# A hybrid decoder layer on one core: the z gates of its linear attention through memory, and joined runs of tile work in its sparse attention

## The chip, the core and the metric

The kernel runs on one core of a Trainium2 chip. The metric is the device time of one execution, in microseconds (us), as the median of several runs.

## What is computed

One step of a decoder layer for 320 tokens: a prompt of 256 and 8 samples of 8 tokens each. The samples have a past of 2048 keys, in caches of 16 pages of 128 keys. Cut to its core, the reference is

```python
u = rmsnorm(x, norm_g) @ w_in                      # 2048 -> 23664 columns, split below
# mixer A, linear attention (gated delta rule): 16 q/k heads, 32 v heads, head dim 128
q, k, v = split(silu(causal_conv4(qkv, conv_state)))
o, s    = gated_delta_chunked(l2norm(q) / 128 ** .5, l2norm(k), v, beta, g, s0)   # chunks of 64 tokens
o_a     = rmsnorm(o, gdn_norm_g) * silu(z)                                        # z: 32 heads
# mixer B, sparse attention: 16 query heads in 4 groups, three kinds of keys, gates g per head
o_cmp   = softmax(q . rmsnorm(compress(k_cmp)) + bias) @ compress(v_cmp)          # pooled blocks of 32, stride 16
o_sel   = softmax(q . k_sel + bias, the 16 best blocks of 64) @ v_sel
o_win   = softmax(q . k_win + bias, last 512 keys) @ v_win
o_b     = (g0 * o_cmp + g1 * o_sel + g2 * o_win) * silu(z_b)
y       = x + (sigmoid(m_a) * (o_a @ w_branch_a) + sigmoid(m_b) * (o_b @ w_branch_b)) @ w_out
```

The new keys and values, the convolution's tails and the states s are outputs too.

## The kernel before

**The projection as filler.** The weight products are most of the work. Each weight tile is split in two parts, whi (a copy rounded to the fast matmul type, on ACT) and wlo (weight less whi, on DVE). A tile of 128 columns over one k-tile of 128 rows then takes three matmuls into the PSUM tile acc, all 320 tokens wide: hhi by whi, hlo by whi, hhi by wlo (hhi and hlo are the two parts of the normed input). With 16 k-tiles a block of 128 columns is 48 of them.

The blocks stand in a queue Q of "slabs", filled by slab(). Four streams serve it, each strictly in order: p_load (the weights' DMAs on SP, three buffers wraw), p_hi, p_lo and p_mm (the matmuls on PE). Each slab has a condition ready: p_mm starts no block until it holds, and what stands behind in Q waits with it. At a block's end a function of the slab takes acc away: take_raw and take_mz copy it to a buffer raw (ACT; four of them, counted by room), and take_mz writes that to memory from POOL's queue; take_g copies it to xp, the convolution's input.

The order of Q is: the heads' gates (bag), q, the six kinds of keys and values, the gates z_b, m_a, m_b (take_mz, to d_mz), half of the z gates (the 16 heads listed in ZS: take_mz, to d_z), and then for each pair j of v heads (j = 0 to 15) a slab of q and k columns, one of v columns and, for j > 0, one of the pair's z columns that are not in ZS. Last come three slabs of m_b, then w_branch_b, w_branch_a and w_out.

**Who sets the order.** Everything else is a set of Python generators (prepare, prompt, compressed, window, two workers of sample, and for each j the streams of the linear attention). Each yields the engine and tiles that it needs next. A planner (Clock and Run) keeps modelled engine times and lets the stream step that can start first; at equal times the rank decides. p_mm has the highest number for a rank: its matmuls come where no other stream can run on PE. So the program order of every engine is fixed when the kernel is built, and at run time each engine works through its row in order. All instructions are recorded by one helper (L330; the DMAs at L298), so the profile's groups are told apart by tiles.

**The linear attention.** For each j: conv (the xp tiles to cv), load_z (reads z_b and the z heads in ZS, line 1616), norms (silu of q, k, v and z; transposes), prep and inverse (the chunks' triangular inverses: long chains of products of 32x32 tiles, ps by T, X, A and TTd), then g2 (the four prompt chunks) and g3 (the samples, which read and write states sS of all 8 sequences: matmuls pu, writes o_s_gdn). pos["g2"] and pos["g3"] count the pairs that are through. The tile z has three buffers. The matmul for the z columns of pair j goes straight into that tile (take_g of kind "z"), so its slab has the condition of line 1597:

```python
okz = lambda f, j=j: pos["g2"] >= j - 2 and pos["g3"] >= j - 2
```

The q/k and v slabs have another, ok: at most four xp tiles at a time.

**The sparse attention.** Part of PE's work here uses a part of its array: tiles of 128 rows by 32 columns (four groups of heads side by side), 64 by 32, 64 by 128 or 32 by 32. A matmul of the projection uses 128 by 128. pooled (line 1158) takes four pages of the compressed cache at a time and multiplies each by the weights Pk to 32 rows of pp: a run of 7 instructions, then three of 4. scores (1291) transposes pages of keys (nt, copied to kT) and multiplies them by the queries: 4 instructions ns for a page, two pages at a time in sample and one in window; after the pages come 4 for the sample's new keys. weighted (1312) does the same with the transposed probabilities pT and pages of values (op), the new values last, from vsS or vwS with 64 rows. In prompt (997) each head's transposed pooled probabilities pcT have 64 rows, and the matmul with vcp uses 64 of the array's rows.

Of the kernel before, what the change touches and what calls it, by code (L numbers as in the profile page):

```python
# [21 lines left out]
P = 128  # L22
# [3 lines left out]
B = 8  # L26
# [16 lines left out]
NWP = 5  # L43
# [392 lines left out]
def step(ctx: ExitStack, tc: tile.TileContext, I, O):  # L436
# [32 lines left out]
    d_z = dpool.tile([len(ZS), P, NT], F32, name="d_z")  # L469
# [328 lines left out]

    room = lambda f: done["taken"] - done["raw"] < NRAW
# [8 lines left out]
    for x in mz[:24 - NM]:  # L808
        w_in(*x)
    for i in range(0, len(ZS), 2):  # L810
        w_in([(OZA + 128 * j, 128) for j in ZS[i:i + 2]], take_mz(d_z, i))
# [20 lines left out]
    vcp = wtab.tile([64, 4, P], F32, name="vcp")  # L832
# [131 lines left out]
    def prompt_compress(tok):  # L964
        V.memset(kcpT, 0.0)
        V.memset(vcp, 0.0)
        for kv, nm in enumerate(("kc", "vc")):
# [22 lines left out]
            else:  # L990
                vp = wps.tile([P, 512], F32, tag="b", name="vp")
                for g in range(4):
                    T.matmul(vp[:32, g * P:g * P + P], pt[:, g * 32:g * 32 + 32], proj[:, 1], start=True, stop=True)
                yield "dve"
                V.tensor_copy(vcp[:32].rearrange("p g d -> p (g d)"), vp[:32])

    def prompt():
        yield lambda: done["names"]
        qp = {}
        for g, tt in ((g, tt) for g in range(4) for tt in range(2)):  # L1000
# [32 lines left out]
            for h in range(4):  # L1033
                T.transpose(tp[:64, h * P:h * P + P], pc[:, h], ident)
            yield "act"
            pcT = wk.tile([64, 512], F32, tag="wpcT", name="pcT")
            S.activation(pcT, tp[:64], AF.Copy)
            ob = wk.tile([P, 4, P], F32, tag="wob", name="ob")
            for h in range(4):
# [38 lines left out]
                T.matmul(op[:, :P], vcp[:, g], pcT[:, h * P:h * P + P], start=False, stop=True)  # L1078
# [73 lines left out]
    cfeed = Feed(cp, "cpg", 6, [page(key, b, 4 * j + i) for b in range(B) for key in ("k_cmp", "v_cmp")  # L1152
# [5 lines left out]
    def pooled(b, kv):  # L1158
        pp = cps.tile([P, 512], F32, tag="a", name="pp")
        for i in range(4):  # L1160
            pg = []
            for _ in range(4):
                pg.append((yield from cfeed.get()))
            yield ("pe", *pg)
            for j in range(4):
                T.matmul(pp[32 * j:32 * j + 32], Pk[:, kv, i], pg[j], start=i == 0, stop=i == 3)
# [3 lines left out]
            cfeed.release(4)  # L1170
# [66 lines left out]
    def select(h):  # L1237
# [17 lines left out]
        for a in (0, 15):  # L1255
            big = cp.tile([P, 2, 450], F32, tag="big", name="big", bufs=1)
            mine, other = bc(sc[:, a:], [[1, 15], [0, 30]]), bc(sc, [[0, 15], [1, 30]])
            v = [big[:, k].rearrange("p (a b) -> p a b", a=15) for k in range(2)]
# [13 lines left out]
    class Env:  # L1272


        def __init__(self, pp, st, tt, nt, pl, n, i, feed):
            self.feed, self.next, self.nt = feed, Next(pp, tt), nt
            self.s = lambda name: pp.tile([P, 512], F32, tag=st, name=name)
            self.t = lambda name: pp.tile([P, 512], F32, tag=tt, name=name, bufs=nt)
            self.x = lambda name: pl.tile([P, 512], F32, tag=f"{name}{i}", name=name, bufs=n)
# [11 lines left out]
    def scores(e, b, npg, dst, kS, finish):  # L1291

        for quad in range(0, npg, 4):
            ns = e.s("ns")
            prev = []
            for p in range(0, 4 + e.nt, e.nt):
                got, now = [], []
                if p < 4:
                    for _ in range(e.nt):
                        got.append((yield from e.feed.get()))  # L1300
                    yield ("pe", *got, e.next)
                    for k, pg in enumerate(got):
                        if k:
                            yield ("pe", e.next)
                        nt = e.t("nt")
                        for g in range(4):
                            T.transpose(nt[:, g * P:g * P + P], pg[:, g * P:g * P + P], ident)
                        now.append(nt)
                        e.feed.release()
                if prev:  # L1310
# [1028 lines left out]
```

## Time and profile before

| | us |
|---|---|
| median of 3 runs | 2661.42 |
| lowest and highest | 2658.48, 2663.15 |
| the profiled execution | 2657.93 |
| its span, first to last instruction | 2655.9 |

The page's rows count instructions as the hardware runs them: a float32 matmul of the sparse or linear attention is two records, one of the projection is one. PE stands for the matmuls and PEld for the loads of their weights; a time such as 1467.6 is microseconds from the span's start. In the span, input and norm take the first 30 us, the sparse attention lies between 30 and about 1100, the linear attention between about 1100 and 2229, and after it only projection is left. "clock" is the TensorE clock granted, as a share of full speed; its mean over the execution was 0.988.

### The profile page before, as it was taken

To read this page: it belongs to the slowest core of one execution; us is meant where nothing else is said; L and a number is where in the kernel's file an instruction comes from. 1 tells how busy PE (TensorE), PEld (TensorE's weight loads), DVE (VectorE), ACT (ScalarE), POOL (GpSimd) and SP (SyncE) were. 2 spreads that over 40 slices of the span, in tenths; PEclk is the share of its full clock that TensorE was granted. 3 is DMA by queue.
4 is the path that set the end of the run, shared out by engine and by line. 5 is a ranking of instruction groups with operands and counts; after the bars stand their busy time and mean duration, and the time that the engine had idled before them with its cause. 6 is when DMAs were issued, how large, how long until landed. Compare 5 with 4: busy or idle time off the path is not lost. (4 is left out here: it accounts for less than half of the span.)

```text
span 2655.9 us, 59457 instructions
## 1 busy us (share of the span) xinstructions
PE 2581.8 (97%) x22228; PEld 2332.5 (88%) x22228; DVE 1648.4 (62%) x4089; ACT 1407.7 (53%) x3290; POOL 398.0 (15%) x967
## 2 busy tenths in 40 slices
PE   7999999999999999999999899989999899999999
PEld 5897788777878888899999699979998789999999
DVE  5554445655556555544887787878878776454543
ACT  5453443434433333345778568777777565444443
POOL 2000011000000000000222343324242322000000
PEclk9999999999999999999999899989999899999999
DMA  6747777898768998765546256545464366656654
GB/s 193 232 156 242 232 238 268 273 322 267 252 207 281 316 359 273 242 195 156 153 152 189 88 179 180 163 131 154 145 189 147 122 195 216 208 180 191 184 191 131
DMA packets 548677, 543.89 MB, mean 205 GB/s; under 512 B 32482, under 2 KB 452499, under 8 KB 548003
## 3 DMA queue, kind: packets, MB, share of 16 engines
q1 hardware_dynamic: 534308, 493.67, 58.3%
q0 software_dynamic: 14080, 46.41, 5.1%
q8 instruction: 175, 2.87, 0.4%
q14 instruction: 114, 0.93, 0.1%
HBM read 470.31 MB, written 69.67 MB: 203 GB/s over the span
## 5 line engine op out<-in xcount | busy, mean ns | idle before, releaser
L330 PE MATMUL acc<-hhi,whi 128*128 128x320 f32 (+1 forms) x3472 | 1146.3, 330 | 1.5 <-ACT hhi L330 1.5
L330 PE MATMUL acc<-hhi,wlo 128*128 128x320 f32 (+1 forms) x3472 | 1075.3, 310 | 0.0
L330 PE MATMUL acc<-hlo,whi 128*128 128x320 f32 (+1 forms) x3472 | 1074.1, 309 | 0.5 <-DVE hlo L330 0.4
L330 ACT ACTIVATE whi<-wraw 128x512 fp32r<-128x512 f32 (+1 forms) x996 | 626.2, 630 | 834.5 <-PE acc L330 792.4
L330 DVE TENSOR_TENSOR wlo<-wraw,whi 128x512 fp32r<-128x512 f32 x992 | 685.4, 694 | 576.3 <-ACT whi L330 545.6
L330 PEld LDWEIGHTS acc<-hhi,whi 128*128 128x128 f32 (+1 forms) x3472 | 654.9, 189 | 70.1 <-issue 57.4
L330 PEld LDWEIGHTS acc<-hlo,whi 128*128 128x128 f32 (+1 forms) x3472 | 655.6, 189 | 7.0 <-issue 2.2
L330 PEld LDWEIGHTS acc<-hhi,wlo 128*128 128x128 f32 (+1 forms) x3472 | 653.5, 188 | 0.0
L330 PE MATMUL acc<-oah,whi 128*128 128x320 f32 x512 | 158.2, 309 | 0.0
L330 PE MATMUL acc<-oal,whi 128*128 128x320 f32 x512 | 158.2, 309 | 0.0
L330 PE MATMUL acc<-oah,wlo 128*128 128x320 f32 x512 | 158.2, 309 | 0.0
L330 POOL CAST vx<-v 32x128 fp32r<-32x128 f32 x256 | 97.8, 382 | 143.7 <-DVE v L330 91.5
L298 POOL DMA_DIRECT2D d_mz<-raw x48 | 26.2, 545 | 605.5 <-ACT raw L330 594.1
L330 DVE SCALAR_TENSOR_TENSOR cv<-xp,cw,cv 128x344 f32<-128x344 f32 x192 | 109.9, 573 | 6.0 <-ACT cv L330 4.7
L330 ACT ACTIVATE kT<-nt 128x512 f32<-128x512 f32 x80 | 47.6, 596 | 109.2 <-PE ns L330 63.4
L330 DVE COPY kT<-nt 128x512 f32<-128x512 f32 x80 | 55.1, 690 | 69.7 <-PE ns L330 51.6
L330 PEld LDWEIGHTS acc<-oah,whi 128*128 128x128 f32 x512 | 96.1, 188 | 0.0
L330 PEld LDWEIGHTS acc<-oal,whi 128*128 128x128 f32 x512 | 96.1, 188 | 0.0
L330 PEld LDWEIGHTS acc<-oah,wlo 128*128 128x128 f32 x512 | 96.1, 188 | 0.0
L330 DVE SCALAR_TENSOR_TENSOR sS<-sS,ends,pu 128x128 f32<-128x128 f32 x256 | 82.8, 338 | 19.0 <-PE pu L330 18.1
L330 PE MATMUL pp<-cpg,Pk 128*32 128x512 f32 x608 | 88.0, 602 | 0.8 <-DMA cpg<-cache_k_cmp 0.7
L330 PE MATMUL nt<-pk_const,spg 128*128 128x128 f32 x512 | 68.5, 275 | 1.2 <-DVE kT L330 0.9
(422 smaller groups left out, 3436.3 us busy)
## 6 DMA issues: line engine op xcount, KB each, us to landing
wraw<-w_in SPq DMA_DIRECT2D x136, 1024.0 KB
wraw<-w_in SPq DMA_DIRECT2D x97, 512.0 KB
cpg<-cache_k_cmp SPq DMA_DIRECT2D x128, 256.0 KB
cpg<-cache_v_cmp SPq DMA_DIRECT2D x128, 256.0 KB
spg<-cache_k_sel SPq DMA_DIRECT2D x128, 256.0 KB
spg<-cache_v_sel SPq DMA_DIRECT2D x128, 256.0 KB
wraw<-w_branch_a SPq DMA_DIRECT2D x32, 1024.0 KB
sS<-state_gdn SPq DMA_DIRECT2D x32, 512.0 KB
```

What stands on the lines that cost most here:

```text
L298: return f(*a, **k)
L330: return f(*a, **k)
```

## The change

**The z gates.** d_z has rows for all 32 heads. The 16 heads that are not in ZS are no longer computed into the tile z. They are computed in eight slabs of two heads each, which stand among the q/k and v slabs (the pair 3, 5 behind those of j = 0, 7 and 9 behind j = 2, and so on to 30 and 31 behind j = 14). Their condition is room: fewer than four raw buffers in use. take_z copies acc to raw, POOL writes it to d_z, and zdone notes the head. load_z reads both heads of a pair with one DMA on SP, once g2 and g3 have come to j - 2 and zdone has both; norms takes them from there. The number of projection matmuls is the same.

**Joined runs.** pooled takes eight pages at a time (8 buffers instead of 6) in runs of 11 and 8 instructions, and gives all eight back at the run's end. scores keeps the transposed keys of four pages in sample (two in window) and multiplies them in one run of 16 instructions (8). The new keys of all samples of a worker come first, in new_scores; in sample POOL copies them to xs. weighted multiplies four pages of values in one run of 16, with the new values' four ahead of the first. In prompt, the pooled probabilities of two heads are transposed at once (16 instructions fewer in all), and vcp is laid out twice, in rows 0 to 63 and 64 to 127 with zeros in the other half, so that its matmul uses the whole array (4 matmuls vp more). qp has one buffer instead of two and is loaded when its group begins. The window's pages go from 5 buffers to 4.

The program's matmuls on PE go from 17904 to 17892. Counted in its order, the runs of instructions that use a part of the array (anything but 128 by 128 or 128 by 64) go from 422 to 288: the pooling's from 62 to 31, those of ns from 101 to 55, those of op in sample and window from 73 to 35, those of op by pcT from 24 to none; in the linear attention they go from 118 to 122, and all others from 44 to 45.

The diff, cut to its core:

```diff
@@ -466,7 +466,7 @@
...
-    d_z = dpool.tile([len(ZS), P, NT], F32, name="d_z")
+    d_z = dpool.tile([32, P, NT], F32, name="d_z")
...
@@ -796,6 +796,14 @@
...
+    zdone = set()
+
+    def take_z(heads):
+        def f(ft, acc):
+            yield from take_mz(d_z, heads[ft])(0, acc)
+            zdone.add(heads[ft])
+        return f
+
...
@@ -807,8 +815,9 @@
...
+    z_pair = lambda x: w_in([(OZA + 128 * j, 128) for j in x], take_z(x))
     for i in range(0, len(ZS), 2):
-        w_in([(OZA + 128 * j, 128) for j in ZS[i:i + 2]], take_mz(d_z, i))
+        z_pair(ZS[i:i + 2])
 
     run.add(gain(), -1)
...
@@ -989,10 +998,12 @@
...
-                for g in range(4):
-                    T.matmul(vp[:32, g * P:g * P + P], pt[:, g * 32:g * 32 + 32], proj[:, 1], start=True, stop=True)
+                for i in range(2):
+                    for g in range(4):
+                        T.matmul(vp[64 * i:64 * i + 32, g * P:g * P + P], pt[:, g * 32:g * 32 + 32], proj[:, 1], start=True, stop=True)
...
@@ -1002,10 +1013,9 @@
...
-                for x in range(len(qp), min(g + 2, 4)):
-                    yield ("sp",)
-                    qp[x] = wwin.tile([P, 4, TP], F32, tag="qp", name="qp", bufs=2)
-                    SY.dma_start(qp[x], d_q[x])
+                yield ("sp", Next(wwin, "qp"))
+                qp[g] = wwin.tile([P, 4, TP], F32, tag="qp", name="qp")
+                SY.dma_start(qp[g], d_q[g])
...
@@ -1030,11 +1040,11 @@
...
-            for h in range(4):
-                T.transpose(tp[:64, h * P:h * P + P], pc[:, h], ident)
+            for h in range(2):
+                T.transpose(tp[:, h * P:h * P + P], pc[:, 2 * h:2 * h + 2].rearrange("p h n -> p (h n)"), ident)
             yield "act"
-            pcT = wk.tile([64, 512], F32, tag="wpcT", name="pcT")
-            S.activation(pcT, tp[:64], AF.Copy)
+            pcT = wk.tile([P, 256], F32, tag="wpcT", name="pcT")
+            S.activation(pcT, tp[:, :256], AF.Copy)
...
@@ -1075,7 +1085,7 @@
...
-                T.matmul(op[:, :P], vcp[:, g], pcT[:, h * P:h * P + P], start=False, stop=True)
+                T.matmul(op[:, :P], vcp[:, h % 2, g], pcT[:, h // 2 * P:h // 2 * P + P], start=False, stop=True)
...
@@ -1149,7 +1159,7 @@
...
-    cfeed = Feed(cp, "cpg", 6, [page(key, b, 4 * j + i) for b in range(B) for key in ("k_cmp", "v_cmp")
+    cfeed = Feed(cp, "cpg", 8, [page(key, b, 4 * j + i) for b in range(B) for key in ("k_cmp", "v_cmp")
...
@@ -1157,17 +1167,18 @@
...
-        for i in range(4):
+        for i in range(0, 4, 2):
             pg = []
-            for _ in range(4):
+            for _ in range(8):
                 pg.append((yield from cfeed.get()))
             yield ("pe", *pg)
-            for j in range(4):
-                T.matmul(pp[32 * j:32 * j + 32], Pk[:, kv, i], pg[j], start=i == 0, stop=i == 3)
+            for k in range(8):
+                j = k % 4
+                T.matmul(pp[32 * j:32 * j + 32], Pk[:, kv, i + k // 4], pg[k], start=i + k // 4 == 0, stop=i + k // 4 == 3)
             if i == 0:
                 for j in range(3):
                     T.matmul(pp[32 * j:32 * j + 32], Pk[:, kv, 4], pg[j + 1], start=False, stop=False)
-            cfeed.release(4)
+            cfeed.release(8)
...
@@ -1288,51 +1300,50 @@
...
+    def new_scores(e, bs, kS, dst):
+
+        yield ("pe", e.sum)
+        ns = e.s("ns")
+        for i, b in enumerate(bs):
+            for g in range(4):
+                T.matmul(ns[32 * g:32 * g + 32, 64 * i:64 * i + 64], qT(b, g), kS[:, g], start=True, stop=True)
+        for i, b in enumerate(bs):
+            yield ("dve", ns)
+            V.scalar_tensor_tensor(dst[:, i], ns[:, 64 * i:64 * i + 64], SCALE, newB[:, 56 - 8 * b:120 - 8 * b], op0=OP.mult, op1=OP.add)
...
         for quad in range(0, npg, 4):
-            ns = e.s("ns")
-            prev = []
...
-                    yield ("pe", *got, e.next)
-                    for k, pg in enumerate(got):
...
+            ks, ns = [], None
+            for p in range(4):
+                pg = yield from e.feed.get()
...
+                e.feed.release()
+                ks.append(e.x("kT", e.nk))
...
+                if len(ks) < e.nk:
+                    continue
+                yield ("pe", *ks, *([] if ns else [e.sum]))
+                ns = ns or e.s("ns")
+                for k, kT in enumerate(ks, p + 1 - e.nk):
+                    for g in range(4):
+                        T.matmul(ns[32 * g:32 * g + 32, k * P:k * P + P], qT(b, g), kT[:, g * P:g * P + P], start=True, stop=True)
+                ks = []
...
-        prev = None
-        for quad in list(range(0, npg + 1, 4)) + [None]:
+
+        pend = []
+        for quad in [npg] + list(range(0, npg, 4)) + [None]:
...
@@ -1341,29 +1352,28 @@
...
-            if prev is not None:
...
-                    yield ("pe", *got, pT)
...
-                        for g in range(4):
-                            T.matmul(op[32 * g:32 * g + 32], pT[:m0, c + 32 * g:c + 32 * g + 32], pg[:m0, g * P:g * P + P],
-                                     start=q0 == 0 and k + i == 0, stop=q0 == npg)
-                        if q0 < npg:
-                            e.feed.release()
+            if quad not in (0, npg):
+                got = []
+                for q0, n0, m0, pT in pend:
+                    for k in range(n0):
+                        got.append(((yield from e.feed.get()) if q0 < npg else vS, pT, k, m0))
+                last = quad is None
+                yield ("pe", *[y[0] for y in got], *[y[3] for y in pend])
+                for i, (pg, pT, k, m0) in enumerate(got):
+                    for g in range(4):
+                        T.matmul(op[32 * g:32 * g + 32], pT[:m0, k * P + 32 * g:k * P + 32 * g + 32], pg[:m0, g * P:g * P + P],
+                                 start=pg is vS, stop=last and i == len(got) - 1)
+                e.feed.release(sum(y[0] is not vS for y in got))
+                pend = []
...
-                pT = e.x("pT")
+                pT = e.x("pT", 2 if npg > 4 else 1) if quad < npg else e.new("pTn")
...
-                prev = quad, n, m, pT
+                pend.append((quad, n, m, pT))
...
@@ -1408,8 +1420,10 @@
...
-        env = Env(sps, "s", "t", 2, smp, 2, "", Feed(smp, "spg", n, req))
-        for b in bs:
+        env = Env(sps, "s", "t", 2, smp, 4, Feed(smp, "spg", n, req))
+        xn = smp.tile([P, len(bs), 64], F32, name="xn")
+        yield from new_scores(env, bs, ksS, xn)
+        for i, b in enumerate(bs):
             yield lambda: done["sel"] > b // 4
...
@@ -1426,11 +1440,15 @@
...
-            yield from scores(env, b, 16, xs, ksS, fin_s)
+            yield ("pool", xn, Place(clock, xs))
+            G_.tensor_copy(xs[:, 2048:], xn[:, i])
...
@@ -1572,15 +1590,9 @@
...
-    def take_g(j, kind, f0=0):
+    def take_g(j, kind):
 
         def f(ft, acc):
-            if kind == "z":
-                z = z_of(j)
-                yield ("act", acc)
-                S.activation(z[:, f0 + ft], acc, AF.Copy)
-                pos["z", j] = pos.get(("z", j), 0) + 1
-                return
             t = g1.tile([P, 347], F32, tag="xp", name="xp", bufs=NXP)
...
@@ -1592,14 +1604,14 @@
...
+    zl = [h for h in range(2 * NG) if h not in ZS]
     for j in range(NG):
...
-        okz = lambda f, j=j: pos["g2"] >= j - 2 and pos["g3"] >= j - 2
         slab(I["w_in"], INW, ((OQ + P * j, P), (OK_ + P * j, P)), KT, hhi, hlo, ok, take_g(j, "c"), xp_enter)
         slab(I["w_in"], INW, ((OV + 256 * j, 256),), KT, hhi, hlo, ok, take_g(j, "v"), xp_enter)
-        zh = [h for h in range(2) if 2 * j + h not in ZS]
-        if zh:
-            slab(I["w_in"], INW, ((OZA + 256 * j + 128 * zh[0], 128 * len(zh)),), KT, hhi, hlo, okz, take_g(j, "z", zh[0]))
+        while zl and zl[0] < 2 * j + 4:
+            z_pair(zl[:2])
+            del zl[:2]
...
@@ -1615,20 +1627,16 @@
...
-        early = [h for h in range(2) if 2 * j + h in ZS]
...
         SY.dma_start(ob, d_ob[j])
-        if early:
-            yield lambda: pos["g2"] >= j - 2 and pos["g3"] >= j - 2
-            yield ("sp",)
-            z = z_of(j)
-            for h in early:
-                SY.dma_start(z[:, h], d_z[ZS.index(2 * j + h)])
-            pos["z", j] = pos.get(("z", j), 0) + len(early)
+        yield lambda: pos["g2"] >= j - 2 and pos["g3"] >= j - 2 and zdone >= {2 * j, 2 * j + 1}
+        yield ("sp",)
+        z = z_of(j)
...
@@ -1677,7 +1685,7 @@
...
 
-        yield lambda: pos.get(("z", j), 0) == 2 and j in hand and len(zob) > j
+        yield lambda: j in hand and len(zob) > j
...
```

PE, in sample, where the keys' scores are taken. Before:

```order
L330 MATMUL nt<-pk_const,spg 128x128 x8
L330 MATMUL ns<-kT,qs 32x128 x8
L330 MATMUL acc<-hhi,whi 128x320
L330 MATMUL acc<-hlo,whi 128x320
L330 MATMUL acc<-hhi,wlo 128x320
...
L330 MATMUL ns<-kT,qs 32x128 x8
```

PE at the same place after:

```order
L330 MATMUL ns<-kT,qs 32x128 x16
L330 MATMUL acc<-hhi,whi 128x320
L330 MATMUL acc<-hlo,whi 128x320
L330 MATMUL acc<-hhi,wlo 128x320
L330 MATMUL nt<-pk_const,spg 128x128 x4
```

Two runs of eight ns have become one of sixteen, and the transposes nt of one page stand alone between projection matmuls.

PE, in the linear attention, around the matmuls pu of a pair's samples (ps are products of the inverse and of the chunks, bank the convolution's transposes). Before, where the z slab of pair 5 stands next in Q:

```order
L330 MATMUL ps<-TTd,A 32x32 x16
L330 MATMUL bank<-pk_const,hist 128x96
L330 MATMUL ps<-T,X 32x32 x16
L330 MATMUL ps<-TTd,A 32x32 x16
L330 MATMUL pu<-vx,k_18464 128x512
L330 MATMUL ps<-T,X 32x32 x16
L330 MATMUL ps<-TTd,A 32x32 x8
L330 MATMUL pu<-vx,k_18464 128x512
L330 MATMUL ps<-X,T 32x32 x8
```

PE around the same work after:

```order
L330 MATMUL ps<-TTd,A 32x32 x16
L330 MATMUL ps<-pk_const,oP 128x128 x4
L330 MATMUL acc<-hhi,whi 128x320
L330 MATMUL acc<-hlo,whi 128x320
L330 MATMUL acc<-hhi,wlo 128x320
L330 MATMUL ps<-T,X 32x32 x16
L330 MATMUL acc<-hhi,whi 128x320
L330 MATMUL acc<-hlo,whi 128x320
L330 MATMUL acc<-hhi,wlo 128x320
L330 MATMUL pu<-vx,k_18163 128x512
```

Before, no projection matmul stands in this row: the four longest rows of PE in the linear attention without one are 165, 164, 120 and 48 instructions long, and all others 20 or less. After, projection matmuls stand in it, and the longest rows without one are 53, 49, 37 and 27.

SP, in the linear attention, between the loads of pair j's z and the weights. Before and then after:

```order
L298 DMA wraw<-w_in 128x8x128 x4
L298 DMA sS<-state_gdn 128x8x128
L298 DMA z<-d_z 128x320
L298 DMA wraw<-w_in 128x8x256
L298 DMA row<-d_gc 128x640
```

```order
L298 DMA sS<-state_gdn 128x8x128
L298 DMA wraw<-w_in 128x8x128 x2
L298 DMA z<-d_z 128x2x320
L298 DMA wraw<-w_in 128x8x128 x2
```

The load of z holds two heads and still stands between loads of weights.

More of the change, by code (lines that the diff above doesn't have):

```diff
@@ L42 @@
 OR = -4
-NWP = 5
+NWP = 4
 SW = ((10, (0, 1, 2, 4)), (10, (3, 5, 6, 7)))
@@ L831, in step @@
     kcpT = wtab.tile([P, 4, 64], F32, name="kcpT")
-    vcp = wtab.tile([64, 4, P], F32, name="vcp")
+    vcp = wtab.tile([P, 2, 4, P], F32, name="vcp")
     zero = x4("zero").rearrange("p (a b) -> p a b", a=2)
@@ L1255, in select @@
         for a in (0, 15):
-            big = cp.tile([P, 2, 450], F32, tag="big", name="big", bufs=1)
+            big = [cp.tile([P, 450], F32, tag=t, name="big", bufs=1) for t in ("c2", "c3")]
             mine, other = bc(sc[:, a:], [[1, 15], [0, 30]]), bc(sc, [[0, 15], [1, 30]])
-            v = [big[:, k].rearrange("p (a b) -> p a b", a=15) for k in range(2)]
+            v = [x.rearrange("p (a b) -> p a b", a=15) for x in big]
             yield "dve"
@@ L1272, in step, with __init__ @@
     class Env:
-        def __init__(self, pp, st, tt, nt, pl, n, i, feed):
-            self.feed, self.next, self.nt = feed, Next(pp, tt), nt
+        def __init__(self, pp, st, tt, nt, pl, nk, feed):
+            self.feed, self.next, self.sum, self.nk = feed, Next(pp, tt), Next(pp, st), nk
             self.s = lambda name: pp.tile([P, 512], F32, tag=st, name=name)
             self.t = lambda name: pp.tile([P, 512], F32, tag=tt, name=name, bufs=nt)
-            self.x = lambda name: pl.tile([P, 512], F32, tag=f"{name}{i}", name=name, bufs=n)
+            self.new = lambda name: pl.tile([64, P], F32, tag=name, name=name)
+            self.x = lambda name, n: pl.tile([P, 512], F32, tag=name, name=name, bufs=n)
     def softmax(x, n, b, br, mx):
@@ L1324, in scores @@
             yield ("dve", ns)
             finish(quad, ns)
-        yield ("pe",)
-        ns = e.s("ns")
-        for g in range(4):
-            T.matmul(ns[32 * g:32 * g + 32, :64], qT(b, g), kS[:, g], start=True, stop=True)
-        yield "dve"
-        V.scalar_tensor_tensor(dst[:, npg * P:npg * P + 64], ns[:, :64], SCALE, newB[:, 56 - 8 * b:120 - 8 * b], op0=OP.mult, op1=OP.add)
     def weighted(e, b, npg, x, vS, op):
-        prev = None
-        for quad in list(range(0, npg + 1, 4)) + [None]:
+        pend = []
@@ L1375, in fin_w @@
                 V.scalar_tensor_tensor(xw[:, :8], ns[:, :8], SCALE, winB, op0=OP.mult, op1=OP.add)
-            yield from scores(wenv, b, 4, xw, kwS, fin_w)
+            yield from new_scores(wenv, (b,), kwS, xw[:, 512:].rearrange("p (a k) -> p a k", a=1))
+            yield from scores(wenv, b, 4, fin_w)
             yield from softmax(xw, 576, b, 2, mx)
+            yield ("pe", wenv.sum)
             op = wenv.s("op")
@@ L1399, in step @@
     wwin = pool(w_ctx, "wwin")
-    wenv = Env(wps, "a", "b", 1, wwin, 1, "", Feed(wwin, "wpg", NWP, [wpage(key, b, p) for b in range(B) for key in ("k_win", "v_win") for p in range(4)]))
+    wenv = Env(wps, "a", "b", 1, wwin, 2, Feed(wwin, "wpg", NWP, [wpage(key, b, p) for b in range(B) for key in ("k_win", "v_win") for p in range(4)]))
     run.add(window())
@@ L1432, in sample @@
             yield from softmax(xs, 2112, b, 1, mx)
-            op = sps.tile([P, 512], F32, tag="s", name="op")
+            yield ("pe", env.sum)
+            op = env.s("op")
             yield from weighted(env, b, 16, xs, vsS, op[:, 0:P])
```

51 lines of the change are left out of this document (16 added, 35 removed).

## The prediction

> **What bounds the kernel now.** The profiled execution took 2657.93 us, its span 2655.9; the median is 2661.42, 3.5 more. I make the sum as a difference and take it off the median. A measurement of this kernel can tell about 0.2% (5 us) from no change.
>
> First the page's busy times and its slices of the span:
>
> ```profile
> PE 2581.8 (97%) x22228; PEld 2332.5 (88%) x22228; DVE 1648.4 (62%) x4089; ACT 1407.7 (53%) x3290; POOL 398.0 (15%) x967
> PE   7999999999999999999999899989999899999999
> PEclk9999999999999999999999899989999899999999
> ```
>
> PE is the bound nearly everywhere, and three slices fall short in busy share and in clock. Whatever PE's program costs is time, so two things can be saved: PE's work, and those holes. The chain of waits gives the projection's price:
>
> ```profile
> 2228.98 312.40 PE acc L330 x2130
> ```
>
> 312.40 / 2130 = 0.1467 us for one acc. Next the windows, cut at the holes (columns: length, busy time of PE, PEld, DVE, ACT and POOL with instructions, clock, DMA share, GB/s), and the same for the tile acc alone:
>
> ```profile
> 30.00:1100.00 1070.00, 1063.98 (x9259) 880.28 (x9262) 582.35 (x1320) 444.45 (x910) 54.49 (x99) 1.00 0.77 257
> 1100.00:1467.60 367.60, 364.30 (x3043) 353.22 (x3031) 238.53 (x578) 230.40 (x554) 65.92 (x187) 1.00 0.58 174
> 1467.60:1505.30 37.70, 26.32 (x310) 20.97 (x310) 29.38 (x107) 18.36 (x64) 15.26 (x40) 0.77 0.30 93
> 1505.30:1770.30 265.00, 261.49 (x2489) 248.23 (x2488) 214.64 (x633) 198.99 (x538) 85.15 (x230) 0.99 0.52 158
> 1770.30:1793.90 23.60, 15.61 (x231) 12.01 (x231) 16.88 (x64) 13.19 (x50) 10.95 (x26) 0.71 0.43 131
> 1793.90:2044.10 250.20, 248.22 (x2386) 236.19 (x2385) 204.04 (x591) 190.72 (x515) 84.38 (x215) 1.00 0.54 166
> 2044.10:2085.50 41.40, 26.95 (x311) 21.59 (x309) 32.52 (x117) 20.00 (x70) 14.70 (x40) 0.75 0.26 79
> 2174.70:2179.40 4.70, 2.12 (x97) 1.75 (x96) 2.52 (x7) 2.17 (x6) 1.43 (x4) 0.81 0.81 273
> ```
> ```profile
> 1467.60:1505.30 37.70, 0.05 (x1) 0.12 (x1) 0.00 (x0) 0.00 (x0) 0.77 0.30 93
> 1505.30:1770.30 265.00, 206.00 (x1200) 179.42 (x1200) 0.00 (x0) 11.40 (x43) 0.99 0.52 158
> 1770.30:1793.90 23.60, 0.06 (x1) 0.08 (x1) 0.00 (x0) 0.51 (x2) 0.71 0.43 131
> 1793.90:2044.10 250.20, 202.28 (x1200) 178.11 (x1200) 0.00 (x0) 11.51 (x43) 1.00 0.54 166
> 2044.10:2085.50 41.40, 0.23 (x3) 0.04 (x1) 0.00 (x0) 0.50 (x2) 0.75 0.26 79
> 2174.70:2179.40 4.70, 0.09 (x1) 0.00 (x0) 0.00 (x0) 0.00 (x0) 0.81 0.81 273
> ```
>
> The four holes (107.4 us together) hold next to no acc; the stretches between them hold 1200 each. Why acc stops is seen where it comes back, at about 1505: g3's last write of the states (POOL), then the copy of a z block.
>
> ```profile
> 1500.71 0.91 POOL L298 DMA_DIRECT2D o_s_gdn<-sS  x1 [1.51 <-DVE sS L330]
> 1521.04 0.42 ACT L330 ACTIVATE z<-acc 128x320 f32<-128x320 f32 x1
> ```
>
> The z slab's condition okz let no projection start until g3 was two pairs behind, and the queue behind it stood too.
>
> **Part one: the z slabs.** The filler moved into the holes costs nothing there that it doesn't save later: every acc done earlier is missing from the tail. What the holes' own work costs in a filled stretch is read from the two filled ones: (265.00 + 250.20 − 2400 × 0.1467) / (1289 + 1186 other records) = 163.1 / 2475 = 0.0659 us a record. The holes hold 949 records, 6 of them acc: 943 × 0.0659 = 62.1 us, so 107.4 − 62.1 = 45 us go. From below: PE's busy time there is 71.0 us, and if filling saved none of it, 36 us go. From above: those 71.0 us ran at clocks around 0.75, at full clock they are 53, and 54 go. The holes' records are mostly 32x32 products, cheaper than the mean, so I take **49 us**, between the two.
>
> The clock gate has a rule in the Trainium skill, "TensorE: Matmul & The Clock Gate", Part 1: a window with PE mostly idle lowers the clock. The trace agrees: 0.71 to 0.81 in the holes, 0.99 to 1.00 around them.
>
> What the new route adds: 16 more copies to raw in place of 16 to z (nothing on ACT), 16 more writes by POOL and z loads of twice the size. The rows for POOL:
>
> ```profile
> L298 POOL DMA_DIRECT2D d_z<-raw x16 | 8.6, 540 | 114.8 <-ACT raw L330 107.5 <-ACT al L330 7.3
> POOL d_mz L298 <- ACT raw L330: 14.7, 4, 5.4
> ```
>
> The issue is 0.54 us. Before it POOL waits for the copy; in the linear attention's last part four such waits took 14.7 us, 3.7 each. Behind it stand POOL's casts vx and the copies of TTf and k, on which g3 and the inverse hang. 16 × (0.54 + 3.7) = 68 us of POOL at most, none to some of it on the path. I take 0: POOL is busy for 85.15 of 265.00, DVE and ACT work meanwhile, and PE has filler to put there. Without that cover it would be up to 68. On SP the load of z waits for d_z and for z's buffer, and behind it stand loads of weights. Three weight buffers hold at least 24 acc each (8 k-tiles of one block), 72 × 0.1467 = 10.6 us of cover; only a wait longer than that costs. I take 0. The bytes (16 × 0.16 MB written and read, 5 MB) fall where the DMA share is 0.52 to 0.58.
>
> **Part two: joined runs.** What leaving full-array work costs is read from two places in PE's timeline, 4 instructions (8 records) and 16 (32), each between acc:
>
> ```profile
> 464.18 0.31 PE L330 MATMUL acc<-hhi,wlo 128*128 128x320 f32 x1
> 464.42 0.43 PE L330 MATMUL ns<-kT,qs 128*32 128x128 f32 x8
> 464.78 0.41 PE L330 MATMUL acc<-hhi,whi 128*128 128x320 f32 x1
> 465.03 0.30 PE L330 MATMUL acc<-hlo,whi 128*128 128x320 f32 x1
> ```
> ```profile
> 918.44 0.31 PE L330 MATMUL acc<-hhi,wlo 128*128 128x320 f32 x1
> 918.68 1.08 PE L330 MATMUL op<-spg,pT 128*32 128x128 f32 x32
> 919.69 0.41 PE L330 MATMUL acc<-hhi,whi 128*128 128x320 f32 x1
> 919.95 0.30 PE L330 MATMUL acc<-hlo,whi 128*128 128x320 f32 x1
> ```
>
> From the acc before to the second acc behind: 0.85 and 1.51 us. Less two acc (0.293): 0.557 and 1.217. The twelve more cost 0.660, 0.055 each; so the visit itself costs 0.557 − 4 × 0.055 = 0.337 us. The program makes 422 visits before and 288 after: 134 × 0.337 = **45 us**. Small terms: 16 fewer transposes, and four more vp, about +1 together at 0.1 us each. Against it, in 16 runs (8 in sample, 8 in window) the new values' 64-row tile now stands ahead of 128-row tiles, a change of tile within the visit. Between 0 and 16 × 0.337 = 5.4; I take 2, since only one edge of a visit is paid. Net **44 us**.
>
> A tile of 128 by 64 is a part of the array too; there are 8 fewer of such runs (57 for 65), tp by pc in prompt:
>
> ```profile
> 719.73 0.62 PE L330 MATMUL tp<-pk_const,pc 128*64 128x128 f32 x4
> 720.11 0.39 PE L330 MATMUL acc<-hhi,whi 128*128 128x320 f32 x1
> 720.33 0.31 PE L330 MATMUL acc<-hlo,whi 128*128 128x320 f32 x1
> ```
>
> The second acc comes 0.22 us behind the first, not the 0.25 to 0.26 behind a 128*32 visit; I give these eight nothing. The Trainium skill, "TensorEngine Tiling (Array Packing)", Key Properties, says that any change of tiling mode drains TensorE. By that rule they would be worth 8 × 0.337 = 2.7 us more.
>
> What the joining adds is waits: a run now needs more pages or copies at once.
>
> ```profile
> cpg<-cache_k_cmp SPq DMA_DIRECT2D x128, 256.0 KB
>   DMA cpg<-cache_k_cmp: 5.6, 9
>   DMA cpg<-cache_v_cmp: 1.4, 3
> 922.00:932.30 10.30, 10.30 (x177) 8.22 (x175) 4.29 (x9) 2.80 (x5) 0.00 (x0) 1.00 1.01 344
> ```
>
> Before, PE waited for pooled's pages 12 times, 7.0 us in all. I take the same again, so 0; the window's eight runs on four values' pages (four buffers, all given back at once) go with it. qp, now loaded when its group begins, is wanted four times; PE has filler meanwhile: 0. POOL's 8 small copies to xs come where POOL is busy for 54.49 of 1070.00: 0.
>
> **Sum.** 49 + 44 = 93 us; 2661.42 − 93 = **2568 us**. Its own range: at best the holes give 54, the joining 46, and PE's remaining idle time in the filled windows (6.0 + 3.3 + 3.5 + 2.0 = 14.8 us) goes too, 2547; at worst the holes give 36 and the joining 40, 2585.
>
> **The rivals.** *The linear attention is bound by its own chain, not by PE's program.* DVE is busy for 81% and 82% of the filled stretches (214.64 of 265.00, 204.04 of 250.20) and for 78% of the holes at 1467 and 2044. Then the holes' saving comes back as waits between matmuls, and only the joining is left: 2661 − 44 = 2617. Against it: PE idles for only 3.5 and 2.0 us in these stretches, so chains and filler run beside each other at that pace already, and 49 us off some 1100 raises DVE's share by under four points. Chance 0.12.
>
> *The joining saves nothing*, since each longer run waits for its last page or copy about as long as the visit it spares: 2661 − 49 = 2612. The planner places a run when it reckons the pages there, and page waits are 7 us now. Chance 0.05.
>
> *The other side: pooled's pages.* All eight buffers come free only at a run's end, and the next run wants all eight, 2.1 MB: 6.1 us at the 344 GB/s above, 8.2 at the sparse attention's mean of 257, twice that if weights share the queue half and half. PE works in order, so everything stands behind that run. There are 31 gaps; from 93 / 31 = 3.0 us of wait in each the change loses. At 4 us: 31 × 4 = 124, 2568 + 124 = 2692. For it: before, 6 buffers left two pages ready beyond each run. Against it: the program has at least 42 acc (6.2 us) and other work in the shortest gap, and mostly far more, 1070 us over 32 runs. Chance 0.05.
>
> *Transposes don't hold the clock up.* In the sparse attention rows of PE without filler stay, more than half of them transposes, the keys' above all:
>
> ```profile
> L330 PE MATMUL nt<-pk_const,spg 128*128 128x128 f32 x512 | 68.5, 275 | 1.2 <-DVE kT L330 0.9
> ```
>
> If the clock fell there to 0.75 as in the holes, these 68.5 us would take a third longer, 23 us, and with as much again of ns and op between them 46: 2591 to 2614. Against it: the window 922 to 932.3 above holds two acc, and otherwise such transposes, ns and op; its clock is 1.00. Chance 0.04. The Trainium skill, "TensorE: Matmul & The Clock Gate", Part 4, states that transposes don't count as work for the clock; the row above speaks against that here.
>
> *Nothing moves*, one gain paid for by another wait: about 2660, chance 0.02.
>
> **The numbers.** The forecast has the rest, 0.72. 2568 is the likeliest. The range, 2545 to 2618, holds it with the first two rivals and most of the clock's; outside are pooled's pages, no change, and a miss below. Faster 0.93, within 0.2% 0.02, slower 0.05.
>
> **What would show it.** Right: in the profile after, acc runs through the former holes, the clock is 1.00 from 30 us on, PE's busy time in the linear attention falls where clock and holes did, the span before the linear attention is shorter by about 44 us, and idle before pp stays under 10 us. Wrong: if PE's idle time between 1100 and 2200 grows behind DVE or POOL (first rival), if idle before pp or ns reaches 30 us or more (second and third), if d_z or z shows in the chain of waits, or if the visits at 128*32 cost other than 0.337 + 0.055 an instruction.

## The result

The changed kernel takes 2573.11 us (median of 4 runs, 2569.02 to 2573.57), the kernel before beside it 2661.19: a ratio of 0.9666, 95% interval 0.965 to 0.9683, 88 us less. The forecast was 93 us less, 2568.

Its page, busy times and slices:

```profile
PE 2518.8 (98%) x22220; PEld 2325.0 (90%) x22220; DVE 1645.7 (64%) x4090; ACT 1400.4 (54%) x3290; POOL 413.2 (16%) x991
PE   7999999999999999999999999999999989999999
PEclk9999999999999999999999999999999999999999
```

PE's busy time fell by 63 us, and the three weak slices in busy share and clock are gone but for one 8 in the busy share. To see where the 84.5 us of span went, the two kernels have to be cut at the same work: the first acc, the last matmul of the sparse attention, the last instruction of PE. The planner now puts 498 more acc into the sparse attention's time, so each part's length says nothing until its acc are taken off. The windows of the kernel before, tile acc alone (length, then PE and PEld with their counts, DVE, ACT, clock, DMA share, GB/s):

```profile
32.40:1109.00 1076.60, 691.50 (x4017) 596.41 (x4017) 0.00 (x0) 34.84 (x83) 1.00 0.77 257
1109.00:2651.40 1542.40, 1259.74 (x7937) 1173.77 (x7935) 7.86 (x16) 60.89 (x198) 0.98 0.55 168
```

and of the changed one:

```profile
32.10:1134.70 1102.60, 772.31 (x4515) 672.26 (x4515) 0.00 (x0) 38.98 (x93) 1.00 0.78 263
1134.70:2566.90 1432.20, 1202.34 (x7439) 1103.93 (x7437) 7.86 (x16) 56.87 (x188) 0.99 0.57 176
```

Less 0.1467 us for each acc (the count of PEld), the sparse attention takes 1076.6 − 4017 × 0.1467 = 487.3 before and 440.3 after: **47.0 less**. The linear attention and all behind it take 378.3 and 341.2: **37.1 less**. I call this the part's own time below.

The largest holes left in the linear attention show in the changed kernel's windows without acc (again the tile acc alone: 2 to 4 records in each):

```profile
1150.97:1157.57 6.60, 0.31 (x4) 0.05 (x2) 0.00 (x0) 0.00 (x0) 0.73 0.75 239
1779.57:1786.40 6.83, 0.31 (x3) 0.17 (x2) 0.00 (x0) 0.48 (x2) 0.93 0.67 215
2070.34:2078.50 8.16, 0.32 (x4) 0.06 (x2) 0.00 (x0) 0.00 (x0) 0.82 0.59 191
2081.86:2087.52 5.66, 0.47 (x2) 0.13 (x2) 0.00 (x0) 0.00 (x0) 0.80 0.54 179
```

27 us in place of 107, with clocks below 1 as in the old ones. The first two are new, and PE's timeline names them: the first matmuls of the linear attention wait for loads, and later a transpose waits for kqP from DVE, while filler stands behind them.

```profile
1152.46 0.43 PE L330 MATMUL bank<-pk_const,c 64*128 64x64 f32 x4 [1.19 <-DMA c<-gdn_conv_w]
1156.95 0.69 PE L330 MATMUL bank<-bag,pk_gini 64*128 64x64 f32 x2 [4.06 <-DMA pk_gini<-c_gini]
1785.57 0.69 PE L330 MATMUL bank<-pk_const,kqP 128*128 128x128 f32 x2 [3.92 <-DVE kqP L330]
```

### The profile page after: what moved, and what is told of

The parts are those of the page before. It is cut to its first block, busy times and chain, and to the rows that moved or that the text cites. A ratio compares the mean times of both kernels' runs of the same rounds, so it can differ in the third digit from the quotient of the medians.

```text
span 2571.4 us, 59460 instructions
## 1 busy us (share of the span) xinstructions
PE 2518.8 (98%) x22220; PEld 2325.0 (90%) x22220; DVE 1645.7 (64%) x4090; ACT 1400.4 (54%) x3290; POOL 413.2 (16%) x991
## 4 chain that ended last, share of the span: by engine, by line
PE 83%; issue 6%; DVE 5%; DMA 2%; POOL 2%; ACT 1%; SPq 0%; DVEq 0%; POOLq 0%; ACTq 0%
PE acc L330 60%; PE ps L330 6%; PE nt L330 3%; PE pp L330 3%; PE op L330 2%; PE ns L330 1%; POOL vx L330 1%; PE bank L330 1%; PE tp L330 1%; DVE wlo L330 1%; PE p L330 1%; PE ms L330 1%; PE pu L330 1%; PE sp L330 1%; DMA spg<-cache_k_sel 1%
## 5 line engine op out<-in xcount | busy, mean ns | idle before, releaser
L330 DVE SCALAR_TENSOR_TENSOR sS<-sS,ends,pu 128x128 f32<-128x128 f32 x256 | 83.2, 339 | 14.5 <-PE pu L330 14.0
L330 PE MATMUL pp<-cpg,Pk 128*32 128x512 f32 x608 | 78.6, 598 | 0.0
L330 PE MATMUL nt<-pk_const,spg 128*128 128x128 f32 x512 | 76.1, 276 | 1.6 <-DMA spg<-cache_k_sel 1.6
```

What stands on the lines that cost most here:

```text
L330: return f(*a, **k)
```

## The experiments

### Each part alone

The z part alone is the hunks on d_z, take_z, z_pair, take_g, the slabs' order, load_z and norms on the kernel before; the joined runs alone are all others.

> The kernel before with only the z part of the change (all z gates through d_z, eight slabs of two heads that wait for a raw buffer alone). Theory (the two parts are independent: the z part fills the holes of the linear attention, the joined runs save visits in the sparse attention): in the profile after, the linear attention's time less its acc at 0.1467 us fell by 37 us, so about 2661 - 37 = 2624, within 5, with the sparse attention as before. Rival (the two parts work on each other: the joined runs make the sparse attention take 498 more acc early, and only that leaves the linear attention its shorter holes): less than 25 saved, 2636 or more.

> The kernel before with only the joined runs, the z slabs as before. Theory: the sparse attention loses 134 + 4 visits at 0.337 us or so, 47 us in the profile after, and the holes of the linear attention (rows of 165, 164, 120 and 48 instructions without acc in its program, as before) stay: about 2661 - 47 = 2614, within 5. Rival (the parts work on each other): 2604 or less, with smaller holes, or 2625 and more.

The z part alone: 2614.73 us (2609.83 to 2617.88), ratio 0.983 (0.9814 to 0.9846), 44 less. The joined runs alone: 2615.54 (2613.06 to 2618.64), ratio 0.9837 (0.9821 to 0.9854), 43 less. Together 87, and the whole change gave 88: the parts are independent as far as the medians tell. The two windows of the z part alone:

```profile
33.30:1110.60 1077.30, 691.22 (x4018) 596.11 (x4018) 0.00 (x0) 34.89 (x83) 1.00 0.76 257
1110.60:2611.60 1501.00, 1275.64 (x7936) 1176.90 (x7935) 7.86 (x16) 61.13 (x198) 0.99 0.57 177
```

The sparse attention's own time is 487.9, unchanged; the linear attention's is 336.9, 41 less. The expectation's 2624 within 5 was too cautious by 9 us: it came from the 37 of the whole change. The wait for kqP is here too (3.92 us, in a row of 6.8 us without acc). The joined runs alone:

```profile
32.30:1131.50 1099.20, 771.28 (x4516) 671.36 (x4516) 0.00 (x0) 38.99 (x93) 1.00 0.78 264
1131.50:2611.20 1479.70, 1190.01 (x7438) 1103.81 (x7437) 7.86 (x16) 56.66 (x188) 0.97 0.54 167
```

436.7 in the sparse attention, 51 less; but 388.7 in the rest, 10 more. PE waits there 3.8 us for pk_gini and 1.1 for the weights of the convolution, as in the change, and not in the z part alone. So in the profiles the joined runs give 51 and take back 10 at and behind the linear attention's start; these waits are half of the 10, and the rest was not traced. That the whole time is the expected 2614 is in part luck: the 51 was forecast as 47, and the 10 not at all.

### Is it the condition, or the way through memory?

Without memory, but with more slack:

```diff
-            zs.append(gh.tile([P, 2, NT], F32, tag="z", name="z", bufs=3))
+            zs.append(gh.tile([P, 2, NT], F32, tag="z", name="z", bufs=4))
-        okz = lambda f, j=j: pos["g2"] >= j - 2 and pos["g3"] >= j - 2
+        okz = lambda f, j=j: pos["g2"] >= j - 3 and pos["g3"] >= j - 3
-    NRAW = 4
+    NRAW = 2
```

(and j - 3 in load_z).

> The kernel before, z columns still straight into the tile z, but z has four buffers instead of three and the slab's condition is j - 3 instead of j - 2; to make room, raw has two buffers instead of four (no joined runs). Theory (the holes come from the condition on g2 and g3, and one pair more of slack is enough; memory is only a way to get the slack): its program has no row without acc longer than 54 instructions in the linear attention, so the linear attention gains as in the change, 37 us: about 2624, if two raw buffers cost nothing in the first 450 us. Rival (it is the way through memory that helps, which takes z's copy and silu apart): no gain, about 2661.

2617.98 us (2613.64 to 2618.79), ratio 0.9843 (0.9826 to 0.9859): as good as the z part alone.

```profile
1109.80:2612.50 1502.70, 1267.43 (x7937) 1172.45 (x7935) 7.86 (x16) 60.79 (x198) 1.00 0.56 173
```

The linear attention's own time is 338.6 (378.3 before). The rival falls: the filler stood still because its condition asked for g3 of two pairs earlier, and one pair more of slack frees about as much as the way through memory did (40 and 41 us), and more than the 37 expected. The other way round, memory with the condition put back:

```diff
-            z_pair(zl[:2])
+            z_pair(zl[:2], lambda f, j=j: room(f) and pos["g2"] >= j - 2 and pos["g3"] >= j - 2)
```

> The changed kernel, but each of the eight later z slabs also waits for g2 and g3 to have come to j - 2, as before (j is the pair behind which it stands); the way through memory and the joined runs stay. Theory (the condition makes the holes): the program has rows of 128, 104, 45 and 33 instructions without acc where the changed kernel has 53, 49, 37 and 27; holes of before cost 107.4 us over 497 instructions, 0.216 each, against 0.125 each in a filled stretch (943 records at 0.0659 over 497), so 0.09 each for 144 more of them: 13 us, about 2586, with clock below 1 in those rows. Rival (the condition does not matter once z goes through memory): 2573, within 3.

2583.64 us (2581.95 to 2585.95), ratio 0.972 (0.9704 to 0.9737) against the change's 0.9666: the condition costs, and of the size expected. The linear attention, and the two long holes that are back in it (the tile acc alone):

```profile
1133.10:2576.90 1443.80, 1195.23 (x7438) 1100.71 (x7437) 7.87 (x16) 56.79 (x188) 0.99 0.56 174
1490.70:1518.80 28.10, 0.35 (x3) 0.12 (x2) 0.00 (x0) 0.50 (x2) 0.70 0.28 83
1838.40:1857.40 19.00, 0.35 (x3) 0.09 (x1) 0.00 (x0) 0.50 (x2) 0.73 0.32 93
```

Its own time is 352.8, 11.6 more than the change (13 expected). It isn't the whole of the old loss; eight slabs at every second pair may meet the condition less often than fifteen did, which was not tried apart.

### Single joins undone

Pooling by four again (the hunks on cfeed and pooled), and the pooled probabilities on 64 rows again (those on vcp, vp, tp, pcT and its op):

> The changed kernel with pooled as before: four pages at a time, 6 buffers, runs of 7 and 4; the other joins and the z route stay. Its program has 30 visits to part of the array more. Theory (a visit costs 0.337 us wherever it is): the sparse attention less its acc takes 30 x 0.337 = 10 us more than the 440 of the changed kernel. Rival (eight pages at once make PE wait for pages, and eat most of what the visits give): within 4 us of it, or less. The whole time says less, since the start of the linear attention may wait more or less for its tables (4 to 6 us).

> The changed kernel with prompt's pooled probabilities as before: one head's 64 rows at a time, a matmul op by pcT of 64 of the array's rows in each of 32 steps, 16 transposes more. Its program has 25 visits more. Theory: 25 x 0.337 + 16 x 0.1 - 4 x 0.1 = 9.6 us more in the sparse attention less its acc, the same for a lone matmul of 64 rows as for a run of 32 columns. Rival (only narrow columns cost; a matmul of 64 rows and 128 columns costs no visit): 1 to 2 us more.

2584.72 us (2579.95 to 2585.55), ratio 0.9721 (0.9707 to 0.9736), and 2586.44 (2583.52 to 2588.23), 0.9725 (0.971 to 0.974); the change has 0.9666. Their sparse attentions, one row each:

```profile
32.30:1130.60 1098.30, 755.02 (x4447) 657.96 (x4447) 0.00 (x0) 38.63 (x92) 1.00 0.79 263
```
```profile
32.90:1137.90 1105.00, 758.15 (x4450) 661.13 (x4450) 0.00 (x0) 38.57 (x92) 1.00 0.78 261
```

445.9 and 452.2 in place of 440.3: 5.6 and 11.9 more. The first lies between theory (10) and rival (under 4), the second is near its 9.6 and far from its rival's 1 to 2. One profile of this stage is good for some 5 us only: seven profiles that have all the joined runs (the change twice, the joined runs alone, the condition put back, and the three other kernels under "A better version") give 434.9 to 440.5, 438.2 in the mean. From that mean the two are 7.7 and 14.0 more. By the ratios, 0.9721 against 0.9666 and (the change once more) 0.9681, the first costs 11 to 15 us, and its linear attention's own time (342.0) is that of the change. So theory fits better than the rival, but one profile doesn't settle it. The rival's mechanism isn't there: PE and its weight loads stood before pp for pages 4.3 us in the change and 7.3 with four pages.

### The price of a visit by itself

Extra float32 matmuls on a spare tile (vo by vw) among the acc of w_branch_a, their results unused. It was run once, and only its trace is used:

```diff
+                    if q["kt"] == 32 and k % 4 == 3 and k < 31:
+                        visit(si - visit.first)
```

> The changed kernel with extra float32 matmuls on a spare tile among the acc of w_branch_a, where PE has nothing else: 16 kinds in 16 blocks, each seven times with 12 acc between. Their results are not used. Read from the trace: time from the acc ahead to the second acc behind, less two acc of 0.1467. Theory (0.337 a visit and 0.055 an instruction of 32 columns): 4, 8, 16 and 20 of 128 rows by 32 columns 0.56, 0.78, 1.22 and 1.44; one alone 0.39; one of 64 rows by 128 columns 0.40 or so; 4 of 64 rows and then 16 of 128 rows 1.44 to 1.8; 128 by 64, transposes or matmuls, no fixed cost beside the same work at 128 by 128. Rival (any change of the tile's size costs 0.337): 128 by 64 costs 0.3 more than 128 by 128, and the mixed run 1.78.

Seven of each kind agree within 0.005 us. Less two acc, from the acc ahead to the second behind:

| 128 rows; N = 128 unless said | us | other tiles | us |
|---|---|---|---|
| 1 by 32 columns | 0.532 | one of 128 by 128, matmul | 0.224 |
| 4 by 32 columns | 0.552 | four of 128 by 128, matmul | 0.892 |
| 8 | 0.772 | four transposes, 128 by 128 | 0.440 |
| 16 | 1.209 | four transposes, 128 by 64 | 0.442 |
| 20 | 1.425 | two matmuls side by side, 128 by 64 | 0.565 |
| 4, N = 512 | 1.192 | one of 64 rows by 128 | 0.610 |
| 8, N = 512 | 2.052 | 4 of 64 rows by 32, then 16 of 128 rows | 1.560 |
| 16 of 32 rows by 32 | 0.580 | 4 of 64 rows by 32 | 0.549 |

4 to 20 lie on 0.334 + 0.0547 n, the forecast's 0.337 + 0.055 n. Three forecasts missed. One alone costs nearly as much as four side by side (0.39 forecast). One of 64 rows (0.40 forecast) costs 0.386 more than one of the whole array, a visit and 0.05. And two matmuls on 128 by 64, for which no fixed cost was forecast, cost 0.12 more than two on the whole array (twice 0.224). How the rows read, for the four transposes on 128 by 64:

```profile
2353.01 0.31 PE L330 MATMUL acc<-oah,wlo 128*128 128x320 f32 x1
2353.15 0.60 PE L330 MATMUL vo<-pk_const,vw 128*64 128x128 f32 x4
2353.51 0.39 PE L330 MATMUL acc<-oah,whi 128*128 128x320 f32 x1
2353.74 0.31 PE L330 MATMUL acc<-oal,whi 128*128 128x320 f32 x1
```

the matmul of 64 rows:

```profile
2388.16 0.31 PE L330 MATMUL acc<-oah,wlo 128*128 128x320 f32 x1
2388.40 0.48 PE L330 MATMUL vo<-vw 64*128 64x128 f32 x2
2388.81 0.41 PE L330 MATMUL acc<-oah,whi 128*128 128x320 f32 x1
2389.06 0.31 PE L330 MATMUL acc<-oal,whi 128*128 128x320 f32 x1
```

The visit's cost shows on both sides: 0.24 from the acc to the first matmul of it instead of 0.14 to 0.15, and 0.25 between the two acc behind it, where the transposes have 0.23 and a row of acc 0.15. The two matmuls on 128 by 64 have 0.24 and 0.25 too: by these edges they are a visit, and the transposes on 128 by 64 are not. A run of mixed tiles is recorded under one name:

```profile
2424.41 0.31 PE L330 MATMUL acc<-oah,wlo 128*128 128x320 f32 x1
2424.65 1.43 PE L330 MATMUL vo<-vw 64*32 64x128 f32 x40
2426.01 0.41 PE L330 MATMUL acc<-oah,whi 128*128 128x320 f32 x1
2426.27 0.31 PE L330 MATMUL acc<-oal,whi 128*128 128x320 f32 x1
```

20 instructions, 1.560: only 0.135 more than 20 of one tile.

### A better version

First, the planner's look at the tables' load:

```diff
-        yield ("pe", clock.last, Place(clock, bank[:, :384]))
+        yield ("pe", clock.last, (clock.w[clock.key(E["selp"])][0] + 3000, "sp"), Place(clock, bank[:, :384]))
```

> The changed kernel with one line of the linear attention's start changed: the planner puts PE's first matmuls with the loaded tables 3 us behind the time at which it reckons the table pk_gini loaded; before, it looked at no load there. 45 more acc (6.6 us) then stand ahead of them. Theory (the changed kernel lost 6 us at 1151 because PE's row stood behind that load while filler was ready): 6 us less than the changed kernel, about 2567, with no wait of PE for pk_gini or the conv weights. Rival (the wait only moves, since conv and everything behind it start later): 2573.

2568.26 us (2563.38 to 2570.34), ratio 0.9655 (0.9642 to 0.9668). The interval overlaps the change's; the profile tells more:

```profile
1136.00:2561.70 1425.70, 1200.86 (x7438) 1102.40 (x7437) 7.86 (x16) 56.82 (x188) 0.99 0.57 177
```

334.7 against 341.2, and no wait for pk_gini: 6.5 less, as expected, in the profile; the medians alone don't show it. With that line in, z without memory, and z through memory in slabs of one head:

```diff
-        while zl and zl[0] < 2 * j + 4:
-            z_pair(zl[:2])
-            del zl[:2]
+        x = [h for h in (2 * j, 2 * j + 1) if h not in ZS]
+        if x:
+            z_pair(x)
```

> The changed kernel once more, to stand beside the next two: 2571 to 2573 if the run of before is at 2659 to 2661.

> The joined runs with the z columns straight into a tile z of four buffers (condition j - 3, raw with two buffers) and the start of the linear attention planned behind its tables. Theory (the condition made the holes, memory is only one way round it; the 5 MB and POOL's 16 writes cost nothing either way): as the changed kernel with awaited tables, whose rows without acc are as short (54 and 32 against 53, 49, 37): 2661 - 93, about 2567, 5 less than the changed kernel. Rival (the way through memory is worth something by itself): 2573 or more.

> The changed kernel with awaited tables, and the later z heads through memory as slabs of one head at each pair's place (as before the change) instead of two heads at every second place, with no condition but room. Its longest rows without acc in the linear attention are 42, 32 and 21 instructions, against 53, 49, 37 and 27. Theory (what is left of the z gain lies in those rows, 0.09 us an instruction): 166 - 74 = 92 instructions fewer, 8 us less than the changed kernel with awaited tables, about 2560. Rival (those rows are as long as the chains behind them, and the time shows up at other instructions): 2567, no difference.

The change again: 2572.38 us (2566.68 to 2576.76), ratio 0.9681 (0.9661 to 0.9702); z without memory 2567.77 (2563.56 to 2574.66), 0.9662 (0.9643 to 0.968), not to be told from it. Single slabs: **2551.13** (2549.35 to 2552.99), ratio **0.9601** (0.9585 to 0.9617), 21 us less than the change on the same chip and clear of both. The linear attentions of the change again, of z without memory and of the single slabs:

```profile
1129.40:2562.00 1432.60, 1203.93 (x7439) 1105.17 (x7437) 7.85 (x16) 56.83 (x188) 0.99 0.57 176
```
```profile
1134.50:2568.40 1433.90, 1196.03 (x7438) 1100.96 (x7437) 7.85 (x16) 56.60 (x188) 0.99 0.55 172
```
```profile
1132.00:2543.20 1411.20, 1200.34 (x7439) 1100.35 (x7437) 7.85 (x16) 56.72 (x188) 1.00 0.58 179
```

341.6, 342.9 and 320.2; with the tables awaited alone it was 334.7. (The profiled execution of z without memory was the slowest of its five, 7 us above their median.) So the single slabs give 14.5, not the 8 that I had priced by the length of rows without acc. The changed kernel's wait of 3.9 us for kqP on DVE at 1780, in a row of 6 instructions only, is missing with them, and all of PE's waits between 1130 and 2090 us fall from 19.2 to 12.7. Where the planner puts such a transpose decides about that wait, not the length of the row, and my price saw none of it. What makes up the rest of the 14.5 was not traced.

z without memory and the single slabs have their z blocks at the same places in Q (they differ in the number of raw buffers too, two and four), and the second is 17 us faster. So the way through memory is not only as good as one pair more of slack: with a slab for each head and no condition on g2 and g3 it frees more. With the condition j - 3 a row without acc of 17.6 us is left at 1645; the longest with single slabs is 6.6. That the condition is what still holds the filler there is likely, but it was not tried apart.

## Why the prediction held, point by point

**The bound and the price of filler** held: PE's program sets the time, and what is left over after 0.1467 for each acc falls by 84 of the span's 84.5 us. The medians have 88, since the profiled execution of the kernel before was 3 us under its median.

**The visits: 45 us forecast for 134.** Right. The program loses 138 in the sparse attention and gains 4 in the linear one; 138 × 0.337 = 46.5, less 2 for mixed tiles, against 47.0 measured there (51 with the joined runs alone; 49.5 between the mean of the seven profiles with the joined runs and that of three without). With a spread of 5 us between profiles the sum holds to that, no closer. The formula stands in a stage that holds nothing else, for 4 instructions and more. The 2 us for 16 changes of tile within a visit are 16 × 0.135 = 2.2. The 8 runs on 128 by 64 taken at nothing: four such transposes cost 0.442 against 0.440 on the whole array. The rule that I set beside it (the Trainium skill, "TensorEngine Tiling (Array Packing)", Key Properties: a change of tiling mode drains TensorE) fits the tiles of 32 columns or 64 rows here; those transposes speak against it, if a transpose to 64 columns counts as a mode of its own, which no run here tells; and within a visit the change from 64 to 128 rows is worth 0.135 and not 0.337.

**The z slabs: 49 us forecast, 41 measured alone, 37 in the change.** The mechanism was right: the condition made the holes (four buffers without memory free about the same time, and the condition put back costs 11.6). What was off is the size: "I take 49 us, between the two". That sum lets all four holes close to the price of a filled stretch and has no term for waits that the planner's new order brings in. The trace shows one in the z part alone: the row of 6.8 us with PE's wait for kqP, as long as most of the 8 us that are missing there. The rows of 49, 53 and 37 instructions that still have no acc, which the program's order showed beforehand, explain little by the prediction's own price: in the change they take 4.15, 8.15 and 5.67 us, 18.0 together, and their 271 records at 0.0659 make 17.9. In the change the joined runs' shift of filler makes PE wait for its tables too (6 us, gained back in the profile by one line of planning), where I had taken the start of the linear attention as unchanged. How the 12 us divide among these was not shown term by term. Nor was the upper bound of 54 a ceiling: with the tables awaited and single slabs the linear attention's own time is 58 less than before.

The prediction sets a rule on windows with PE mostly idle beside the holes and says that the trace agrees. Its own rows have PE busy for 70, 66, 65 and 45% of the four holes, so the trace shows clocks of 0.71 to 0.81 with less idle time than that. No term of the sum hangs on it.

**The costs taken at 0.** POOL's writes, z's loads and the 5 MB: the way with and without memory, both with the joined runs and awaited tables, can't be told apart (0.9662 without, 0.9655 with), and with single slabs the way through memory is the faster one. In the changed kernel's trace no instruction is listed as waiting for d_z's writes or z's loads. Pages: PE and its weight loads stood for them for 4.3 us, 7.0 before.

**The rivals.** The linear attention's own chain does hold PE at places (3.9 us for kqP from DVE), but it took back a small part of the z slabs' 49 us. The joining did save; pooled's pages didn't come late; the clock was 1.00 over the sparse attention. The sign "the clock is 1.00 from 30 us on" was not quite met: it is 0.99 over the linear attention and what follows, and 0.73 to 0.93 in the holes left.

**A sign that was badly put**: "the span before the linear attention is shorter by about 44". It is 26 longer, since 498 more acc stand in it. Only the time less acc can be compared.

In the profiles the two errors, 12 too much for z and 3 too little for the joining, left 93 at 84; the medians have 88. That the sum came so close is in part luck: the errors have opposite signs.

## What to carry to other kernels

Where one engine runs a queue of filler in order, look first for the condition that stops the head of the queue. Here it cost 40 us at least: a buffer more, or memory between, gave these back, and memory with smaller slabs gave 58. Work on a part of TensorE's array is priced by the visit and by the instruction, so joining runs pays by the number of visits saved, and can be summed beforehand. Where a planner spreads filler, compare stages by their time less the filler, take several profiles where a few us matter, and look for new waits where its order changed.

## What the runs showed of the hardware

Between the projection's matmuls a visit to tiles of 128 rows by 32 columns costs 0.334 us and 0.055 for each instruction of N = 128, for 4 to 20 of them (0.215 for N = 512), and a single one costs about as much as four side by side (0.532 and 0.552). Transposes on 128 by 64 cost no visit (four took 0.442, on the whole array 0.440), while two matmuls side by side on the same tile size took 0.565, against twice 0.224 on the whole array; whether it is the kind of work or the second tile's place that makes this difference was not tried. A change of tile within a visit, from 64 by 32 to 128 by 32, cost 0.135.
